# Attention pool of a hybrid encoder: another tile layout, and the last head pair's order of work

## The chip, the cores and the metric

The kernel runs on one core of a Trainium2 chip. The metric is the device time of one execution in microseconds; before the change the median of three runs was 2669.86 us (2669.14 to 2674.19). A core has five engines that run their own instruction streams: PE (TensorE, matmuls; PEld are its weight loads), DVE (VectorE), ACT (ScalarE), POOL (GpSimd) and SP, which here only issues transfers. Operands of matmuls lie in SBUF, results in eight PSUM banks.

## The reference, cut to what matters

Two layers, sequence 1024, width 1024, all in float32:

```
h = rms_norm(x); p = h @ W_in
y_m = 4 heads of a bidirectional mLSTM          (width 512)
y_a = 8 heads x 64 of dilated attention         (width 512):
      rotary q, k; three patterns (window, dilation) = (128,1), (512,4), (2048,16),
      merged by their softmax denominators
x = x + concat(y_m, y_a) @ W_out
x = x + relu(rms_norm(x) @ W_up)^2 @ W_down     (inner width 4096)
```

and a last RMSNorm. The result has the shape of x.

## The kernel before, in words

Everything is kept transposed: 128 channels in the partitions, the sequence along a row. A float32 weight or activation is split into a high part in a faster matmul type and the rest; a product is three matmuls, high x high, high x rest and rest x high. `wsplit` (L77) splits a weight tile: ScalarE casts it (wh, L81), GpSimd subtracts (wl, L83); there are three buffers of each. `operand` and `parts` (L739 to L747) split an activation of 128x1024: ScalarE casts (L742), VectorE subtracts (L743).

A layer runs: norm, gates and four mLSTM heads (pool `mp`), then eight attention heads as four pairs (pool `ap`), then the output projection and four chunks of up and down projection (pool `up`). `ap` and `up` lie over the same stretch of SBUF; a tile of the later pool waits only for those of the earlier pool that it overlaps. Tiles get their places in the order of their first use; `order` (L51) makes the first ones by name ahead of that.

The output projection and the feed-forward part use seven half-size products where eight would be plain (`seven`, L803). Their weights are loaded by `fetch` on SP's queue (L766), and sums of weight blocks are formed by `plus` (L770), an accumulating transfer that GpSimd issues. Two of the seven products of the output projection need only mLSTM outputs; `out_early` (L867) makes them as fillers of the last attention pair, 32 steps of three matmuls each. The other five run after the pair, starting with `products(w1, operand(Y[1][0]))`, then w2, w0, w1 with its second block, and w2 again. `Y[1]` holds the attention outputs, the later half of its tiles those of the last two pairs.

A pair (`a_pair`, L570) has eight steps T of 128 queries. A step makes scores for two heads (`a_scores`), the softmax rows `sm` (VectorE with mask and minimum L604, ScalarE exponential L606, VectorE reciprocal L607 and scaling L608), the weighting of the step before (`take1`, L580), some fillers, and then eight transposes of `sm` (L620), whose results go to `p1` by ScalarE (L622) and, rearranged, to `p23` by VectorE (L623). After the steps come the last `take1` and two output groups `o2` (L640) for the dilated patterns, each added into y by VectorE (L645). `a_vt` transposes the values at the start of a pair (L560). Fillers in the first three pairs are the next pair's q, k and v projection, 48 steps of three matmuls; `a_split` splits the next pair's q and k.

Within the pairs TensorE keeps the written order (`in_order`). Everything else is ordered by a planner that simulates the engines: an instruction goes into its engine's stream when the simulation has it ready, so work without an open dependency can move ahead of where it is written.

Of the kernel before, what the change touches and what calls it, by code (L numbers as in the profile page):

```python
# [12 lines left out]
F32 = mybir.dt.float32  # L13
F32R = mybir.dt.float32r
# [14 lines left out]
NFF = FF // P  # L29
FCH = 8  # L30
NCH = NFF // FCH
POS = 1
SQ = 2
NC = S // P
EPS = 1e-6
# [9 lines left out]
class Trunk:  # L45
# [505 lines left out]
    def a_vt(self, vt, ap, fill):  # L551
        nc = self.nc
        v1 = ap.tile([P, NC + 1, P], F32, name="v1", tag="v1", bufs=1)
        v23 = ap.tile([P, 8, P], F32, name="v23", tag="v23", bufs=1)
        jobs = [(v1, i, vt[:, i * P:(i + 1) * P]) for i in range(NC + 1)]
        jobs += [(v23, 2 * rr + jt, vt[:, 64 + 512 * jt + rr:64 + 512 * (jt + 1):4]) for rr in range(4) for jt in range(2)]
        for lo, n in ((0, 4), (4, 4), (8, 1), (9, 4), (13, 4)):
            pt = self.mx.tile([P, 4, P], F32, name="pt", tag="t", bufs=2)
            for i in range(n):
                nc.tensor.transpose(pt[:, i], jobs[lo + i][2], self.ident)  # L560
            dst, j = jobs[lo][0], jobs[lo][1]
            nc.scalar.copy(dst[:, j:j + n], pt[:, :n])
            fill(1)
        return v1, v23

    def a_pair(self, p, qkv, ops, ap, more, nxt=None, each=5):

        nc = self.nc
        y = self.ytile(MH + p)
        late = None  # L570

        def fill(n):
            for _ in range(n):
                next(more, None)

        def take1(T, o1, p1s):
            for b in range(2):
                for g in range(4):
                    gp = slice(32 * g, 32 * g + 32)
                    nc.tensor.matmul(o1[gp, T % 4], v1[:, T + b, gp], p1s[g // 2][:, b], start=b == 0, stop=b == 1)  # L580
            if T % 4 == 3:
                yv = y[T // 4].rearrange("p (T i r) -> p T r i", T=4, r=4)
                ov = o1.rearrange("p T (r i) -> p T r i", r=4)
                for i in range(4):
                    nc.scalar.copy(yv[:, i], ov[:, i])

        if p == 0:
            fill(2)
            v1, v23 = self.a_vt(qkv[2], ap, fill)
        for T in range(NC):  # L590
            pss = [self.mx.tile([P, 2, 256], F32, name="ps", tag="s", bufs=2) for _ in range(2)]
            self.a_scores(qkv, ops, pss, T)
            if T == 0:
                if p > 0:
                    v1, v23 = self.a_vt(qkv[2], ap, fill)
                p23 = [ap.tile([P, 2, 4, NC, 32], F32, name=f"p23{h}", tag=f"p23{h}", bufs=1) for h in range(2)]
            sms = []
            for h in range(2):
                sm = ap.tile([P, 2, 256], F32, name="sm", tag="sm", bufs=2)
                nm, l = [ap.tile([P, 1], F32, name=n_, tag=n_, bufs=2) for n_ in ("nm", "l")]  # L600
                b0 = 32 * (NC - 1 - T)
                x = self.am[:, b0:b0 + 256]
                mk = bass.AP(x.tensor, x.offset, [x.ap[0], (480 - b0, 2), (1, 256)])
                nc.vector.tensor_tensor_reduce(out=sm, in0=pss[h], in1=mk, op0=ALU.add, op1=ALU.min, scale=-0.125,  # L604
                                               scalar=3e38, accum_out=nm)
                nc.scalar.activation(sm, sm, AF.Exp, scale=-1.0, bias=nm, accum_out=l)  # L606
                nc.vector.reciprocal(l, l)  # L607
                nc.vector.tensor_scalar(out=sm, in0=sm, scalar1=l, scalar2=None, op0=ALU.mult)  # L608
                sms.append(sm)
            if late:  # L610
                take1(*late)
            fill(each if T < NC - 1 else each - 2)
            if T % 4 == 0:
                o1 = self.mx.tile([P, 4, P], F32, name="o1", tag="o", bufs=1)
            p1s = []
            for h in range(2):
                pt = self.mx.tile([P, 4, P], F32, name="pt", tag="t", bufs=2)
                smf = sms[h].rearrange("p g w -> p (g w)")
                for i in range(4):
                    nc.tensor.transpose(pt[:, i], smf[:, i * P:(i + 1) * P], self.ident)  # L620
                p1 = ap.tile([P, 2, P], F32, name="p1", tag="p1", bufs=2)
                nc.scalar.copy(p1, pt[:, 2:4])  # L622
                nc.vector.tensor_copy(p23[h][:, :, :, T], pt[:, 0:2].rearrange("p j (r i) -> p j r i", r=4))  # L623
                p1s.append(p1)
            late = T, o1, p1s
        if nxt and POS == 0:
            self.a_split(nxt, ops)
        fill(1)
        take1(*late)
        if nxt and POS == 1:  # L630
            self.a_split(nxt, ops)
        fill(3)
        for g in range(2):
            o2 = self.mx.tile([P, 2, 256], F32, name="o2", tag="o", bufs=1)
            for rr in range(2):
                r = 2 * g + rr
                for jt in range(2):
                    for g4 in range(4):
                        gp = slice(32 * g4, 32 * g4 + 32)
                        nc.tensor.matmul(o2[gp, rr], v23[:, 2 * r + jt, gp],  # L640
                                         p23[g4 // 2][:, jt, r].rearrange("p T i -> p (T i)"),
                                         start=jt == 0, stop=jt == 1)
            for t in range(2):
                yg = y[t].rearrange("p (j r) -> p r j", r=4)[:, 2 * g:2 * g + 2]
                nc.vector.tensor_tensor(out=yg, in0=o2[:, :, t * P:(t + 1) * P], in1=yg, op=ALU.add)  # L645
            if nxt and POS == 2 + g:
                self.a_split(nxt, ops)
            fill(3 if g == 0 else 48)


    def layer(self, L, xT):
# [36 lines left out]
                    pass  # L688
        with tc.tile_pool(name=f"ax{L}", bufs=1, space=PSUM, reuse_waits="tile") as self.mx:
            with tc.tile_pool(name=f"ap{L}", bufs=1, reuse_waits="tile") as ap:  # L690
                self.order(ap, (("p230", 2 * S, 1), ("rp", HALF, 2), ("qq1", S, 1), ("kk1", S, 1)))
                ks = [ap.tile([P, S + P], F32R, name="ks", tag=f"ks{h}") for h in range(2)]
                qd = [ap.tile([P, S], F32R, name="qd", tag=f"qd{h}") for h in range(2)]
                ql = [ap.tile([P, S], F32R, name="ql", tag=f"ql{h}") for h in range(2)]
# [12 lines left out]
                with self.in_order():  # L707
                    for p in range(AH // 2 - 1):
                        nxt = []
                        self.a_pair(p, qkv, ops, ap, self.a_qkv(L, p + 1, hs, r, tabs, ap, nxt), nxt)  # L710
                        qkv = nxt
                    x2, early = [self.yb("x2") for _ in range(KD)], []
                    for o in range(KD):
                        nc.gpsimd.dma_start(x2[o], (a["x"] if L == 0 else self.xd)[:, o])
                    self.a_pair(AH // 2 - 1, qkv, ops, ap, self.out_early(L, x2, early), each=4)
        with tc.tile_pool(name=f"up{L}", bufs=1, reuse_waits="tile") as self.up:
            self.order(self.up, (("T", S, 4), ("sq", HALF, SQ)))
            with tc.tile_pool(name=f"dn{L}", bufs=1, space=PSUM, reuse_waits="tile") as self.dn:
                acc, op = self.out_proj(early)
                for c in range(NCH):  # L720
                    u, op = self.up_proj(L, c, acc, op)
                    op = self.down_proj(L, c, x2, u, op)
# [79 lines left out]
    def seven(self, src, B, op, take, nxt, early=False, end=None):  # L802
# [2 lines left out]


        (B11, B12), (B21, B22) = B
        T, T3 = [[self.up.tile([P, 2, HALF], F32, name="T", tag="T", bufs=4) for _ in range(2)] for _ in range(2)]
        w0 = self.fetch("w0", src, 0, 0)
        w1 = self.fetch("w1", src, 0, 1)  # L810
        w2 = self.fetch("w2", src, 1, 0)
        addto = lambda w, m, h: lambda q: self.plus(w[q], src(q, m, h))
        if early:
            chain = P5 = None
            for q in range(4):
                addto(w0, 1, 0)(q)
                addto(w2, 1, 1)(q)
                addto(w2, 0, 0)(q)
        else:
            chain = self.products(w0, op, True, then=addto(w0, 1, 0))  # L820
            op = self.operand(B21)
            for q in range(4):
                addto(w2, 1, 1)(q)
            take(1, chain)
# [150 lines left out]
    def final(self, x2):  # L975
# [33 lines left out]
        def end(w, parts):  # L1009
            ws = []  # L1010
            for q in range(4):
                s = self.up.tile([P, 2, 4, P], F32R, name="s", tag="T", bufs=4)
                wh, wl = s[:, 0], s[:, 1]
                nc.scalar.copy(wh, w[q])
                nc.gpsimd.tensor_tensor(out=wl, in0=w[q], in1=wh.bitcast(F32), op=ALU.subtract)
                ws.append((wh, wl))
# [132 lines left out]
```

## Time and profile before

| | |
|---|---|
| runs | 2669.86 us median, 2669.14 to 2674.19 |
| profiled execution | 2674.39 us, span 2672.6 us, mean granted TensorE clock 0.976 |
| PE busy | 2475.1 us (93%) |
| PEld busy | 1958.6 us (73%) |
| DVE busy | 1962.1 us (73%) |
| ACT busy | 1266.9 us (47%) |
| POOL busy | 1406.8 us (53%) |
| transfers | 214.08 MB, mean 80 GB/s |

The span is the part of an execution from its first to its last instruction. Busy time of an engine leaves out waits, branches and the issue of transfers on SP. In layer 0 the attention pairs run from some 385 to 626 us, in layer 1 from some 1707 to 1947 us; the last pair is 560 to 626 and 1883 to 1947, and the output projection follows it.

### The profile page before, as it was taken

The page shows a single profiled execution, that of the slowest core. Times are in us where ns is not written, and L with a number is a line of the kernel's source. Part 1 is how long each engine was busy: PE and PEld are TensorE (multiplying, and loading weights), DVE is VectorE, ACT ScalarE, POOL GpSimd, SP SyncE. Part 2 cuts the span into 40 slices and gives each one's busy share as a digit, 9 for nine tenths or more (in the row PEclk, how much of TensorE's full clock was granted, in tenths as well). Part 3 has the DMA queues.
Part 4 walks back from the last instruction along what each step waited for, and adds up shares of the span by engine and source line. Part 5 has one row for each costly group of instructions (what it writes and reads, how often), then busy time and mean ns, then how long its engine had stood idle before and what let it go on. Part 6 is the DMA issues. An engine that isn't in the chain of part 4 may idle for free. (4 is left out here: it accounts for less than half of the span.)

```text
span 2672.6 us, 36085 instructions
## 1 busy us (share of the span) xinstructions
PE 2475.1 (93%) x13508; PEld 1958.6 (73%) x13508; DVE 1962.1 (73%) x2456; ACT 1266.9 (47%) x2076; POOL 1406.8 (53%) x1135
## 2 busy tenths in 40 slices
PE   7989989996999999999989898999979999999997
PEld 5777766664778878788767777666657788887876
DVE  7877666586877686967878776566768867768587
ACT  5433344453654545445444334444446445454544
POOL 5333322235576677766654333223266666767765
PEclk9999999998999999999999999999989999999999
DMA  3001100035455455555321111001264555556553
GB/s 133 28 28 32 36 30 25 21 111 127 103 111 107 100 110 112 108 112 115 87 71 32 32 32 38 21 25 51 78 142 95 113 113 107 110 103 111 110 102 85
DMA packets 113327, 214.08 MB, mean 80 GB/s; under 512 B 13424, under 2 KB 15616, under 8 KB 113152
## 3 DMA queue, kind: packets, MB, share of 16 engines
q0 software_dynamic: 46912, 93.06, 21.0%
q1 hardware_dynamic: 66240, 118.71, 14.6%
q8 instruction: 107, 1.75, 0.3%
q14 instruction: 68, 0.56, 0.1%
HBM read 203.33 MB, written 8.39 MB: 79 GB/s over the span
## 5 line engine op out<-in xcount | busy, mean ns | idle before, releaser
L83 POOL TENSOR_TENSOR wl<-w,wh 128x512 fp32r<-128x512 f32 x484 | 777.9, 1627 | 287.7 <-ACT wh L81 286.9
L794 PE MATMUL ph<-b,wh 128*128 128x512 f32 x2240 | 694.3, 391 | 5.9 <-ACT wh L81 5.9
L81 ACT CAST wh<-w 128x512 fp32r<-128x512 f32 x484 | 298.4, 618 | 433.6 <-PE ph L794 118.8
L794 PEld LDWEIGHTS ph<-b,wh 128*128 128x128 f32 x2240 | 422.5, 189 | 95.2 <-ACT wh L81 7.8
L794 PE MATMUL ph<-b,wl 128*128 128x512 f32 x1120 | 441.0, 394 | 13.4 <-POOL wl L83 13.1
L83 POOL TENSOR_TENSOR wl<-wr,wh 128x512 fp32r<-128x512 f32 x132 | 200.1, 1517 | 464.1 <-ACT wh L81 379.2
L794 PE MATMUL pj<-b,wh 128*128 128x512 f32 x1224 | 382.9, 394 | 12.5 <-ACT wh L81 12.5
L91 PE MATMUL pj<-hh,wh 128*128 128x512 f32 x896 | 371.4, 415 | 17.5 <-DVE z L174 10.6
L93 PE MATMUL pj<-hh,wl 128*128 128x512 f32 x896 | 359.5, 401 | 0.9 <-POOL rs L213 0.6
L92 PE MATMUL pj<-hl,wh 128*128 128x512 f32 x896 | 359.8, 402 | 0.0
L743 DVE TENSOR_TENSOR b<-T,b 128x1024 fp32r<-128x1024 f32 x148 | 247.6, 1677 | 135.2 <-ACT b L742 131.5
L794 PEld LDWEIGHTS pj<-b,wh 128*128 128x128 f32 x1224 | 232.0, 190 | 63.8 <-ACT wh L81 14.2
L794 PEld LDWEIGHTS ph<-b,wl 128*128 128x128 f32 x1120 | 211.3, 189 | 67.8 <-POOL wl L83 24.4
L794 PE MATMUL pj<-b,wl 128*128 128x512 f32 x612 | 241.4, 394 | 17.8 <-POOL wl L83 17.8
L91 PEld LDWEIGHTS pj<-hh,wh 128*128 128x128 f32 x896 | 172.4, 192 | 67.0 <-issue 13.9
L93 PEld LDWEIGHTS pj<-hh,wl 128*128 128x128 f32 x896 | 171.9, 192 | 36.7 <-POOL rs L213 1.0
L92 PEld LDWEIGHTS pj<-hl,wh 128*128 128x128 f32 x896 | 172.6, 193 | 30.0 <-issue 0.5
L742 ACT CAST b<-T 128x1024 fp32r<-128x1024 f32 x148 | 155.5, 1051 | 38.4 <-PE ph L794 13.6
L770 POOL DMA_DIRECT2D w<-w_down x128 | 115.9, 936 | 75.7 <-PE pj L794 27.8
L794 PEld LDWEIGHTS pj<-b,wl 128*128 128x128 f32 x612 | 116.2, 190 | 46.2 <-POOL wl L83 22.2
L606 ACT ACTIVATE sm<-sm,nm 128x512 f32<-128x512 f32 x128 | 91.7, 718 | 113.8 <-DVE nm L604 113.8
L770 POOL DMA_DIRECT2D w<-w_up x128 | 113.3, 911 | 59.7 <-POOL wl L83 22.4
(256 smaller groups left out, 4296.7 us busy)
## 6 DMA issues: line engine op xcount, KB each, us to landing
w<-w_up SPq DMA_DIRECT2D x128, 256.0 KB, 2.7
w<-w_up POOLq DMA_DIRECT2D x128, 256.0 KB, 4.1
w<-w_down SPq DMA_DIRECT2D x128, 256.0 KB, 2.7
w<-w_down POOLq DMA_DIRECT2D x128, 256.0 KB, 4.3
wr<-w_in SPq DMA_DIRECT2D x116, 256.0 KB, 2.7
w<-w_out SPq DMA_DIRECT2D x32, 256.0 KB, 5.1
w<-w_out POOLq DMA_DIRECT2D x32, 256.0 KB, 6.1
wr<-w_out SPq DMA_DIRECT2D x16, 256.0 KB, 2.8
```

The costliest lines, as they stand in the source:

```text
L81: nc.scalar.copy(wh, raw)
L83: nc.gpsimd.tensor_tensor(out=wl, in0=raw, in1=wh.bitcast(F32), op=ALU.subtract)
L91: nc.tensor.matmul(ps, wh[:, j, :], xh[:, sl], start=start, stop=False)
L92: nc.tensor.matmul(ps, wh[:, j, :], xl[:, sl], start=False, stop=False)
L93: nc.tensor.matmul(ps, wl[:, j, :], xh[:, sl], start=False, stop=stop)
L606: nc.scalar.activation(sm, sm, AF.Exp, scale=-1.0, bias=nm, accum_out=l)
L742: nc.scalar.copy(hi, src)
L743: nc.vector.tensor_tensor(out=lo, in0=src, in1=hi.bitcast(F32), op=ALU.subtract)
L770: self.nc.gpsimd.dma_start(w, src, accum_op=ALU.add)
L794: nc.tensor.matmul(out, a[:, k, :], b, start=new and k + i == 0, stop=k + i == 5, skip_group_check=not new)
```

## The change

The pools are laid out otherwise, the last pair makes its scores one step ahead, and the fillers are spread otherwise. Places are in columns of four bytes per partition, as the order of tiles gives them:

| columns | `ap` before | `up` before | `ap` after | `up` after |
|---|---|---|---|---|
| 0 to 2048 | p230 | T | p230 | T3 |
| 2048 to 3072 | rp | T | rp | w1 (first two tiles) |
| 3072 to 4096 | qq1 | T | qq0 | w1 (last two) |
| 4096 to 5120 | kk1 | sq | kk0 | T |
| 5120 to 6144 | ks0 | w0 | ks0 | T |
| 6144 to 8192 | ks0, ks1, qd0 | w0, w1 | ks0, ks1, qd0 | w2 |
| 8192 to 10240 | qd0, qd1, ql0 | w1, w2 | qd0, qd1, ql0 | w0 |
| 10240 to 11264 | ql0, ql1 | w2 | ql0, ql1 | sq |

The last pair uses qq1 and kk1, which move behind ql1; qq0 and kk0 are those of the pair before. `rp` held temporaries of the rotary step and now also the `sm` of odd steps of the last pair.

In `a_pair` the softmax part of a step becomes `weights(T)`, the transposes `turn(T, sms)`. In the last pair `weights(T + 1)` stands before the fillers and transposes of step T, and the second head's copy into `p23` goes to ScalarE. Fillers of the last pair: none in `a_vt`, three in each of eight steps, two before the last `take1`, three after it and three between the output groups (before: five, four per step and the rest where it came until the 32 were used up). Pairs 1 and 2 have five in the last step (before three), and two, one and one at the end (before one, three and three); all pairs have three in `a_vt` (before five), and pair 0 four ahead of it (before two). The second output group takes its bank from the tag "t", not "o". In the output projection w0 is fetched last, and its accumulating transfers stand behind those of w2.

```diff
-        for lo, n in ((0, 4), (4, 4), (8, 1), (9, 4), (13, 4)):
+        for lo, n, m in ((0, 4, 1), (4, 4, 1), (8, 1, 0), (9, 4, 1), (13, 4, 0)):
...
-            fill(1)
+            fill(m)
...
+        def weights(T):
             pss = [self.mx.tile([P, 2, 256], F32, name="ps", tag="s", bufs=2) for _ in range(2)]
             self.a_scores(qkv, ops, pss, T)
...
-                sm = ap.tile([P, 2, 256], F32, name="sm", tag="sm", bufs=2)
+                sm = ap.tile([P, 2, 256], F32, name="sm", tag="rp" if last and T % 2 else "sm", bufs=2)
...
+        def turn(T, sms):
...
-                nc.vector.tensor_copy(p23[h][:, :, :, T], pt[:, 0:2].rearrange("p j (r i) -> p j r i", r=4))
+                dst, src = p23[h][:, :, :, T], pt[:, 0:2].rearrange("p j (r i) -> p j r i", r=4)
+                if not last or h == 0:
+                    nc.vector.tensor_copy(dst, src)
+                else:
+                    nc.scalar.copy(dst, src)
...
+        if p == 0:
+            fill(4)
+            v1, v23 = self.a_vt(qkv[2], ap, fill)
+        sms = weights(0)
+        if p > 0:
+            v1, v23 = self.a_vt(qkv[2], ap, (lambda n: None) if last else fill)
+        p23 = [ap.tile([P, 2, 4, NC, 32], F32, name=f"p23{h}", tag=f"p23{h}", bufs=1) for h in range(2)]
+        for T in range(NC):
+            if not last:
+                if T > 0:
+                    sms = weights(T)
+            elif T + 1 < NC:
+                ahead = weights(T + 1)
+            if late:
+                take1(*late)
+            fill((5 if T < NC - 1 or p > 0 else 3) if not last else 3)
+            if T % 4 == 0:
+                o1 = self.mx.tile([P, 4, P], F32, name="o1", tag="o", bufs=1)
+            late = T, o1, turn(T, sms)
+            if last:
+                sms = ahead
+        fill(2)
+        take1(*late)
+        if nxt:
             self.a_split(nxt, ops)
-        fill(3)
+        fill(1 if not last else 3)
         for g in range(2):
-            o2 = self.mx.tile([P, 2, 256], F32, name="o2", tag="o", bufs=1)
+            o2 = self.mx.tile([P, 2, 256], F32, name="o2", tag=("o", "t")[g], bufs=g + 1)
...
-            fill(3 if g == 0 else 48)
+            fill((1 if not last else 3) if g == 0 else 48)
...
-                self.order(ap, (("p230", 2 * S, 1), ("rp", HALF, 2), ("qq1", S, 1), ("kk1", S, 1)))
+                self.order(ap, (("p230", 2 * S, 1), ("rp", HALF, 2), ("qq0", S, 1), ("kk0", S, 1), ("ks0", S + P, 1),
+                                ("ks1", S + P, 1), ("qd0", S, 1), ("qd1", S, 1), ("ql0", S, 1), ("ql1", S, 1),
+                                ("qq1", S, 1), ("kk1", S, 1)))
...
-            self.order(self.up, (("T", S, 4), ("sq", HALF, SQ)))
+            self.order(self.up, (("T3", S, 2), ("w1", HALF, 4), ("T", S, 2), ("w2", HALF, 4), ("w0", HALF, 4),
+                                 ("sq", HALF, SQ)))
...
-        T, T3 = [[self.up.tile([P, 2, HALF], F32, name="T", tag="T", bufs=4) for _ in range(2)] for _ in range(2)]
-        w0 = self.fetch("w0", src, 0, 0)
+        T, T3 = [[self.up.tile([P, 2, HALF], F32, name="T", tag=tag, bufs=2) for _ in range(2)] for tag in ("T", "T3")]
+        if not early:
+            w0 = self.fetch("w0", src, 0, 0)
...
         if early:
             chain = P5 = None
+            w0 = self.fetch("w0", src, 0, 0)
+            for q in range(4):
+                addto(w2, 1, 1)(q)
+                addto(w2, 0, 0)(q)
             for q in range(4):
                 addto(w0, 1, 0)(q)
-                addto(w2, 1, 1)(q)
-                addto(w2, 0, 0)(q)
```

## Rows read from the trace of the kernel before

**Rows 1.** Chain of waits: start us, us, what; feed-forward part of layer 1.
```profile
2062.64 32.64 PE ph L794 x144
```

**Rows 2.** Waits of PE, 1883 to 1981 (layer 1): us in total, times, longest.
```profile
PE pj L794 <- POOL wl L83: 6.3, 1, 6.3
PE pj L794 <- ACT wh L81: 6.2, 1, 6.2
PE ph L794 <- ACT wh L81: 2.9, 1, 2.9
PE pt L620 <- DVE sm L608: 2.3, 2, 1.9
PE pt L620 <- DVE l L607: 1.8, 1, 1.8
PE o L640 <- DVE y L645: 1.3, 1, 1.3
PE o L640 <- ACT y L585: 1.2, 1, 1.2
PE ph L794 <- POOL wl L83: 0.6, 1, 0.6
```

**Rows 3.** Waits of PE, 560 to 660 (layer 0), the first of four alike.
```profile
PE pj L794 <- POOL wl L83: 6.2, 1, 6.2
```

**Rows 4.** Timeline, handover of layer 1: start us, us, work, [idle before <-releaser].
```profile
1932.38 1.11 PE L620 MATMUL pt<-ident,sm 128*128 128x128 f32 x8
...
1933.76 34.15 SPq L766 DMA_DIRECT2D w<-w_out  x16
...
1934.29 1.11 PE L548 MATMUL ps<-kk,qq 64*32 64x256 f32 x16
...
1944.75 1.93 PE L640 MATMUL o<-p,v 128*32 128x256 f32 x32 [1.33 <-DVE y L645]
1946.74 1.12 DVE L645 TENSOR_TENSOR y<-o,y 128x256 f32<-128x256 f32 x2 [2.14 <-PE o L640]
...
1951.29 1.04 ACT L742 CAST b<-T 128x1024 fp32r<-128x1024 f32 x1 [1.23 <-DVE T L752]
1952.24 1.66 ACT L81 CAST wh<-w 128x512 fp32r<-128x512 f32 x3
...
1952.94 9.85 POOL L83 TENSOR_TENSOR wl<-w,wh 128x512 fp32r<-128x512 f32 x3 [11.56 <-ACT wh L81]
...
1957.99 1.22 DVE L743 TENSOR_TENSOR b<-T,b 128x1024 fp32r<-128x1024 f32 x1
1960.38 0.80 PE L794 MATMUL pj<-b,wl 128*128 128x512 f32 x1 [6.25 <-POOL wl L83]
...
1962.74 3.50 POOL L770 DMA_DIRECT2D w<-w_out  x4
...
1975.15 0.62 ACT L81 CAST wh<-w 128x512 fp32r<-128x512 f32 x1 [5.14 <-DMA w<-w_out]
```

**Rows 5.** Tile w, 1933.7 to 1941: twelve fetches, four accumulating transfers.
```profile
DMA to landing us min/median/max: 2.9/7.5/11.5
```

**Rows 6.** Busy time by window: PE, PEld, DVE, ACT, POOL, granted clock, DMA, GB/s.
```profile
1883.00:1947.00 64.00, 56.71 (x545) 38.83 (x537) 47.38 (x113) 26.77 (x68) 13.82 (x16) 0.97 0.35 89
1946.70:2022.00 75.30, 59.30 (x241) 47.66 (x242) 53.80 (x52) 40.76 (x60) 47.12 (x37) 0.89 0.56 120
1946.70:2038.10 91.40, 72.13 (x290) 56.43 (x290) 69.01 (x63) 54.28 (x82) 59.27 (x47) 0.91 0.58 118
```

**Rows 7.** Line L770, 1880 to 1920: three accumulating transfers in the last pair.
```profile
DMA to landing us min/median/max: 3.9/4.1/4.1
```

**Rows 8.** Groups of ACT, 1883 to 1947: busy us, mean ns, idle before.
```profile
L562 ACT COPY v<-pt 128x512 f32<-128x512 f32 x4 | 2.3, 583 | 3.1 <-PE pt L560 3.1
```

**Rows 9.** Waits of PE, 1700 to 1882 (pairs 0 to 2 of layer 1).
```profile
PE pt L620 <- DVE sm L608: 11.8, 6, 3.6
PE o L640 <- DVE y L645: 2.3, 3, 1.3
```

More of the change, by code (lines that the diff above doesn't have):

```diff
@@ L31 @@
 NCH = NFF // FCH
-POS = 1
 SQ = 2
@@ L562, in a_vt, with a_pair @@
             nc.scalar.copy(dst[:, j:j + n], pt[:, :n])
-            fill(1)
+            fill(m)
         return v1, v23
-    def a_pair(self, p, qkv, ops, ap, more, nxt=None, each=5):
+    def a_pair(self, p, qkv, ops, ap, more, nxt=None):
         nc = self.nc
         y = self.ytile(MH + p)
-        late = None
+        late, last = None, nxt is None
         def fill(n):
@@ L585, in take1 @@
                     nc.scalar.copy(yv[:, i], ov[:, i])
[L587 to L590, printed above, removed]
+        def weights(T):
             pss = [self.mx.tile([P, 2, 256], F32, name="ps", tag="s", bufs=2) for _ in range(2)]
             self.a_scores(qkv, ops, pss, T)
[L593 to L596, printed above, removed]
             sms = []
             for h in range(2):
-                sm = ap.tile([P, 2, 256], F32, name="sm", tag="sm", bufs=2)
+                sm = ap.tile([P, 2, 256], F32, name="sm", tag="rp" if last and T % 2 else "sm", bufs=2)
                 nm, l = [ap.tile([P, 1], F32, name=n_, tag=n_, bufs=2) for n_ in ("nm", "l")]
@@ L609, in a_pair @@
                 sms.append(sm)
[L610 to L614, printed above, removed]
+            return sms
+        def turn(T, sms):
             p1s = []
@@ L622, in a_pair @@
                 nc.scalar.copy(p1, pt[:, 2:4])
-                nc.vector.tensor_copy(p23[h][:, :, :, T], pt[:, 0:2].rearrange("p j (r i) -> p j r i", r=4))
-                p1s.append(p1)
-            late = T, o1, p1s
-        if nxt and POS == 0:
-            self.a_split(nxt, ops)
[L628 to L631, printed above, removed]
-        fill(3)
+                dst, src = p23[h][:, :, :, T], pt[:, 0:2].rearrange("p j (r i) -> p j r i", r=4)
[3 more added lines that the diff above has]
+                    nc.scalar.copy(dst, src)
+                p1s.append(p1)
+            return p1s
+        if p == 0:
[22 more added lines that the diff above has]
+        if nxt:
+            self.a_split(nxt, ops)
+        fill(1 if not last else 3)
         for g in range(2):
-            o2 = self.mx.tile([P, 2, 256], F32, name="o2", tag="o", bufs=1)
+            o2 = self.mx.tile([P, 2, 256], F32, name="o2", tag=("o", "t")[g], bufs=g + 1)
             for rr in range(2):
@@ L645, in a_pair @@
                 nc.vector.tensor_tensor(out=yg, in0=o2[:, :, t * P:(t + 1) * P], in1=yg, op=ALU.add)
-            if nxt and POS == 2 + g:
-                self.a_split(nxt, ops)
-            fill(3 if g == 0 else 48)
+            fill((1 if not last else 3) if g == 0 else 48)
     def layer(self, L, xT):
@@ L714, in layer @@
                         nc.gpsimd.dma_start(x2[o], (a["x"] if L == 0 else self.xd)[:, o])
-                    self.a_pair(AH // 2 - 1, qkv, ops, ap, self.out_early(L, x2, early), each=4)
+                    self.a_pair(AH // 2 - 1, qkv, ops, ap, self.out_early(L, x2, early))
         with tc.tile_pool(name=f"up{L}", bufs=1, reuse_waits="tile") as self.up:
-            self.order(self.up, (("T", S, 4), ("sq", HALF, SQ)))
+            self.order(self.up, (("T3", S, 2), ("w1", HALF, 4), ("T", S, 2), ("w2", HALF, 4), ("w0", HALF, 4),
+                                 ("sq", HALF, SQ)))
             with tc.tile_pool(name=f"dn{L}", bufs=1, space=PSUM, reuse_waits="tile") as self.dn:
@@ L1011, in end @@
             for q in range(4):
-                s = self.up.tile([P, 2, 4, P], F32R, name="s", tag="T", bufs=4)
+                s = self.up.tile([P, 2, 4, P], F32R, name="s", tag=("T", "T3")[q // 2], bufs=2)
                 wh, wl = s[:, 0], s[:, 1]
```

## Prediction

> **What bounds the kernel now.** I read the page's engine table first, then TensorE's waits stretch by stretch, then the timeline where they are longest, then busy time by window. The table shows TensorE busy for most of the span, so the kernel can only win where TensorE waits, or runs at its lower clock. In the chain of waits the feed-forward part shows 144 matmuls of 128x512 in 32.64 us without a break, 0.2267 us from start to start [rows 1]; that is my price for a matmul. The largest breaks stand at one place per layer, the handover from the last attention pair to the output projection. In layer 1 TensorE waits there 6.2 us for a cast of a weight (wh), 6.3 us for the rest of the same weight (wl), then 2.9 and 0.6 us for the next product's weights [rows 2], 16.0 us in sum; layer 0 repeats it, its wait for wl is 6.2 us [rows 3].
>
> The timeline says why [rows 4]. The last score matmuls of the pair start at 1934.29 and end at 1935.40, and only at 1933.76 does SP begin the twelve weight fetches, since their slots lay on the score operands; with the first accumulating transfers they land up to 11.5 us after issue [rows 5]. The last matmuls of the pair end at 1946.7. VectorE then works without a gap to 1959.2, two adds of the output and ten differences and subtractions in SBUF that had no slot or operand before. ScalarE casts the first weights at 1952.24, behind casts of these operands. GpSimd begins wl at 1952.94 and needs 9.85 us for three; TensorE gets the first of them at 1960.38, 1.2 us after VectorE's run has ended. Meanwhile four accumulating transfers stand behind those wl in GpSimd's queue and are issued from 1962.74, so the second product's weights are cast only at 1975.15, after 5.14 us of waiting on a transfer.
>
> The five steps of the projection in this stage are 240 matmuls, 240 x 0.2267 = 54.4 us at full rate. From 1946.7 to their end at 2022.0 they take 75.3 us: 20.9 us lost, 16.0 of them waits and 4.9 at the lower clock (granted 0.89 over the window [rows 6]: part of the time at 1.2 GHz, after the waits).
>
> **The change part by part** (per layer; rows of layer 1).
>
> *Layout and order of loads.* After the change half of w1 lies on the key/query tiles of the pair before (free early), half on the tile "rp", which now holds softmax rows of the last odd step; w2 and w0 lie on score operands as before, T on kk0 and ks0. From the last scores to the end of the pair there lay 11.3 us, of which 4.4 us waits (1.9, 1.2, 1.3 [rows 2]), so 6.9 us of work. After it there lie the same 6.9 us, eight transposes more (1.1 us [rows 4]) and 14 fillers of three matmuls (3+3+2+3+3, 0.68 us each, 9.5 us): 17.5 us. So w2 and w0 are fetched 17 us before the pair ends. The "rp" half of w1 comes free at the last transposes, 9.3 us before the end (8 fillers 5.4, two output groups of 1.93). With the median landing of 7.5 us all are there in time. The eight accumulating transfers of w2 are two in series, 4.1 us landing each in the last pair [rows 7]: 17.5 - 7.5 - 8.2, ready about when the pair ends, and needed 48 matmuls (10.9 us) later. The issues themselves (0.87 us each on GpSimd by the row of four, twelve of them) go into a stretch where GpSimd is busy 13.8 of 64 us [rows 6].
>
> So at the end of the pair w1 is split for three of four tiles (three wh/wl buffers), the differences into T are done, and the first six matmuls have operands from older pairs. What is late next: the operand of the last pair itself, an add 0.56, a cast 1.04, a subtraction 1.22 us and the handoffs between them, some 3.4 us after the end against 1.4 us of matmuls that don't need it: 2 us at most, less if the planner puts other products between. Then wl of the fourth tile: its buffer comes free 2.7 us after the end and VectorE then has some 8 us of subtractions (this operand 1.1, an unused one 2.3, the next difference and its operand 4.6). I take 2 us for that; bounds are 0 (GpSimd gets in between) and 6.3 (as now [rows 2]). Left of 20.9 us: 4. **Gain 16.9 us.**
>
> *A rule on this.* The first of the three wl lasts from 1952.94 to TensorE's start at 1960.38, 7.4 us under VectorE's run; the other two share the 2.4 us left [rows 4]. The Trainium skill, "SBUF — State Buffer", section "Who interferes with whom", says that a VectorE operation with two SBUF inputs and a GpSimd operation that reads SBUF exclude one another, and that the second to issue blocks until the first finishes. By that the wl would have waited for one subtraction, 1.1 us, not for six; the trace disagrees on the length. By the rule the residue would be 3 us and not 4, and the gain 1 us more a layer.
>
> *Last pair.* Waits now: 1.8 and 2.3 us on softmax rows, 1.2 on a ScalarE copy, 1.3 on the adds between the two output groups, 6.6 in sum [rows 2], and about 1 us of low clock after them (granted 0.97 over 64 us [rows 6] could be worth 1.9; I take half). Scores a step ahead give the softmax a whole step; the 32 fillers reach to the end instead of running out in step 7; the second output group gets a bank of its own. VectorE is busy 47.4 of 64 us there [rows 6] and gives one of two strided copies per step to ScalarE (busy 26.8), so on the mean it is not the limit; in the first half, where each four fillers bring four adds into x and not two, the mean says little. New: the 17 transposes of the values stand without fillers; five copies of 0.58 us and less [rows 8] pace them, some 3 us with handoffs, of which TensorE's own work hides perhaps half: 1.5 us. Another 1.5 us I leave for waits in the dense steps (bounds 0 and the 4.1 of today on softmax rows). **Gain 7.6 - 3 = 4.6 us.**
>
> *Pairs 0 to 2.* Waits now 14.1 us, 11.8 on softmax rows and 2.3 on the adds between output groups [rows 9]. The 2.3 go. Pairs 1 and 2 have two more fillers in step 7 (1.4 us of cover each, 2.8). Against it there is one filler (0.68) where three stood ahead of the first output group, which waits for ScalarE's copies (the 1.2 us of rows 2 came with none): 0.7 us each, 2.1; and fewer fillers among the value transposes, 0.5 each in two pairs. 2.3 + 2.8 - 2.1 - 1.0: **gain 2 us**, bounds -2 and 6.
>
> *Behind the handover.* The same VectorE work must fit in less time. From the end of the pair to the sum of squares at 2038.1 it is busy 69.0 of 91.4 us [rows 6]. With 16.9 us less it has 74.5, of which some 5 us of work has gone ahead into the pair (four operations of 1.2 us into T and the older half of the operand): 64 of 74.5. Tight, with GpSimd contending; I take 2.5 us given back (bounds 0 and 10).
>
> *At nothing:* T3 and T as two tags (the same four buffers), the s tiles, the moved constant, w0 fetched last: it is used third, 22 us after the handover. If that cover were gone, w0 would cost its landing, 7.5 us at most.
>
> **Sum:** 16.9 + 4.6 + 2 - 2.5 = 21.0 a layer, 42.0 in both. The profiled execution took 2674.39 us (span 2672.6 and 1.8 around it); 2674.4 - 42.0 = 2632.4. The median of the runs is 2669.86, 4.5 lower; by the same difference 2627.9, and I say 2628.
>
> **Rivals.** *VectorE bounds the stretch up to the norm* (18%). For it: 64 of 74.5 us, and GpSimd wants the same memory ports, as rows 4 show from its side. Against it: in the feed-forward part the same pair runs beside a full TensorE. Price 7 to 10 given back instead of 2.5: 2628 + 2 x 6 = 2640, up to 2645.
> *Half the handover stays* (14%): the "rp" half of w1 and ScalarE's order make wl late again, behind VectorE's run. For it: 7.4 us once already. Against: 9.3 us of lead. The 6.3 us wait and its low clock stay, 9 us less gain a layer: 2646.
> *Everything goes* (11%): handover and last pair without residue, nothing given back, pairs 6: 20.9 + 7.6 + 6 = 34.5 would be the limit; some 30 a layer give 2610.
> *It does not do what it says* (3%): the planner leaves the fetches where they are; only pairs and banks remain, 2 us a layer, 2666.
> *Slower* (4%): the accumulating transfers, now inside the pair, stand in GpSimd's queue ahead of a filler's wl. TensorE keeps its written order there, so it waits for the filler while GpSimd waits for a fetch. The wait is at worst a fetch and two accumulating transfers in series, 11.5 + 4.1 + 4.1 = 19.7 us [rows 5, 7]; with 4.9 us of low clock behind it 24.6 a layer, more than the 21.0 gained: 2669.9 + 7 = 2677. It decides from 21 us of loss per layer. Against it: wl of the fillers are due before the last scores, and the fetches start only there.
> The Trainium skill, "SBUF — State Buffer", section "SBUF: two separate sides", has a rule of that kind: transfers issued from GpSimd starve while VectorE runs operations that take the shared ports. The three accumulating transfers now in the last pair, amid softmax scaling, land in 4.1 us, no later than 0.2 us behind the fastest [rows 7]; by that row it doesn't bite here, and I add no chance for it.
>
> **How the numbers follow.** Forecast 50%, 2617 to 2640 by the bounds of its residues. Range 2610 to 2650: outside lie the far half of "everything goes", the edges of the two middle rivals, and the last two. A measurement of this kernel can tell 0.2%, 5.3 us. Faster than 2664.5: all but the last two, 0.93; within: 0.03; slower: 0.04.
>
> **What would show it.** Right: w_out fetches issued before the last pair's second output group; the two waits of six us gone and less than 5 us of waiting between the pair's end and the end of the projection; the granted clock there near 1.0; no wait for the adds between output groups. Wrong: a wl over 4 us at the handover; a wait of more than 5 us at the norm's matmuls; fillers waiting for wl in the last pair; a wait for copies above 1 us ahead of each first output group.

## The result and the profile after

The changed kernel took 2657.1 us (median of 6 runs, 2649.64 to 2660.53) beside 2670.69 us for the kernel before: ratio 0.9944, interval [0.9929, 0.9958]. It is faster, by 14 us and not by 42; the time lies above the predicted range. The profiled execution has a span of 2651.2 us, 21.4 less than before.

The table cuts the span at two places per layer: E, where the last output matmul of the last pair ends, and N, where the matmuls with ones of the norm behind the projection start again after their wait for VectorE's sum acc (both from the timeline, in us). "Start to E" and "N to E" hold the pairs, "E to N" the handover and the projection.

| kernel | start to E, layer 0 | E to N, layer 0 | N to E, layer 1 | E to N, layer 1 | rest |
|---|---|---|---|---|---|
| before | 626.3 | 90.3 | 1230.2 | 91.5 | 634.5 |
| after | 614.6 | 89.6 | 1221.3 | 91.6 | 634.2 |
| e1_pair_only | 612.4 | 91.8 | 1218.9 | 92.1 | 634.3 |
| e2_layout_only | 623.5 | 91.8 | 1226.0 | 89.7 | 636.7 |
| e3_rows_kk0 | 615.0 | 92.8 | 1214.6 | 91.5 | 636.9 |
| e4_wh_first | 612.5 | 84.4 | 1220.1 | 82.7 | 635.4 |
| e5_order_all | 611.8 | 82.5 | 1217.8 | 86.3 | 637.6 |
| e6_pair_wh_first | 614.1 | 83.3 | 1216.9 | 82.4 | 634.5 |
| e7_pair_order_all | 613.8 | 83.7 | 1219.7 | 81.6 | 637.1 |
| e8_order_fill | 616.3 | 82.8 | 1220.8 | 82.6 | 635.4 |
| e9_before_wh_first | 623.2 | 82.3 | 1225.0 | 82.8 | 636.6 |
| e10_t_after | 612.5 | 79.8 | 1220.1 | 80.9 | 633.5 |

After against before: all that was won was won ahead of E, 11.7 and 8.9 us. E to N, from which the prediction took 14.4 us a layer, moved by -0.6 and +0.1.

The waits of TensorE in the last pair and the handover of layer 1, which answer to [rows 2] (us in total, times, longest):
```profile
PE pj L812 <- ACT wh L80: 4.0, 1, 4.0
PE ph L812 <- ACT wh L80: 3.8, 1, 3.8
PE ph L812 <- DVE x L818: 3.4, 1, 3.4
PE pt L559 <- ACT v L561: 1.9, 1, 1.9
PE pj L812 <- POOL wl L82: 1.0, 1, 1.0
```
Layer 0 has the same five (4.0, 2.8, 3.6, 1.9 and 1.0 us), where 6.2 us for wl stood before [rows 3]. The pair's own waits (6.6 us) are down to 1.9 us in the value transposes, and TensorE waits for no add between the output groups any more. At the first product 5.0 us are left of 12.5. But the wait at the second product (ph for wh) is 3.8 us where it was 2.9, and a wait of 3.4 us for VectorE's adds is new. Pairs 0 to 2 of layer 1, against [rows 9]:
```profile
PE pt L613 <- DVE sm L602: 8.5, 5, 2.9
PE o L657 <- ACT y L585: 2.4, 3, 1.5
PE pt L559 <- ACT v L561: 1.1, 2, 0.6
```
The timeline of the handover in layer 1, against [rows 4]:
```profile
1914.83 21.17 SPq L784 DMA_DIRECT2D w<-w_out  x15
...
1923.55 1.93 PE L657 MATMUL o<-p,v 128*32 128x256 f32 x32
...
1926.19 1.04 ACT L760 CAST b<-y 128x1024 fp32r<-128x1024 f32 x1 [7.85 <-DVE y L662]
1926.59 1.22 DVE L770 TENSOR_TENSOR T<-y 128x1024 f32<-128x1024 f32 x1
...
1928.85 1.66 ACT L80 CAST wh<-w 128x512 fp32r<-128x512 f32 x3
...
1929.51 0.73 PE L812 MATMUL pj<-b,wh 128*128 128x512 f32 x2 [4.02 <-ACT wh L80]
1929.54 6.10 POOL L82 TENSOR_TENSOR wl<-w,wh 128x512 fp32r<-128x512 f32 x3 [18.34 <-ACT wh L80]
...
1931.26 0.80 PE L812 MATMUL pj<-b,wl 128*128 128x512 f32 x1 [1.02 <-POOL wl L82]
...
1935.58 2.62 POOL L788 DMA_DIRECT2D w<-w_out  x3
...
1947.92 0.62 ACT L80 CAST wh<-w 128x512 fp32r<-128x512 f32 x1 [5.32 <-DMA w<-w_out]
```
The fetches begin at 1914.8, 10.7 us before E at 1925.5, and not 17. The first two tiles of w1 lie on `rp`, and w2 and w0 stand behind them in SP's one queue, so all twelve wait for the last transposes; the waits of SP's queue, 1912 to 1925:
```profile
SPq L784 <- PE pt L613: 3.3, 1, 3.3
```
The row to look at is the cast of `b` at 1926.19: ScalarE sat idle for 7.85 us until VectorE's `y`, the result of the pair's last matmuls. Only behind it, and behind a cast of T, do the casts of w1 come, without a wait of their own: the weights were there (fetched from 1914.8, landed at most 6.0 us after issue). The differences into T, which VectorE makes, also begin only behind `y`, at 1926.59. GpSimd in turn sat 18.3 us until the first wh. When the weights landed decides nothing here; where their casts stand in ScalarE's order does. The kernel before has the same row:
```profile
1947.38 1.04 ACT L742 CAST b<-y 128x1024 fp32r<-128x1024 f32 x1 [5.95 <-DVE y L645]
```
Busy time of layer 1 by window, against [rows 6] (us; busy PE, PEld, DVE, ACT, POOL; granted clock, DMA share, GB/s). First the kernel after, cut at the second product's first matmul, then the kernel before with the same cut:
```profile
1925.50:1948.60 23.10, 14.27 (x49) 10.95 (x49) 19.97 (x15) 9.15 (x13) 15.20 (x13) 0.83 0.61 125
1948.60:2000.80 52.20, 47.01 (x192) 37.60 (x193) 43.16 (x38) 31.26 (x49) 31.45 (x27) 0.95 0.56 118
1925.50:2017.00 91.50, 74.40 (x290) 57.36 (x290) 78.92 (x63) 53.49 (x82) 59.56 (x51) 0.93 0.60 120
```
```profile
1946.70:1975.80 29.10, 13.74 (x48) 10.38 (x48) 18.52 (x17) 9.83 (x14) 18.07 (x12) 0.77 0.62 128
1975.80:2022.00 46.20, 45.56 (x193) 37.27 (x194) 35.29 (x35) 30.93 (x47) 29.05 (x25) 0.96 0.51 115
```
Up to the second product the changed kernel is 6.0 us shorter (23.1 against 29.1), and it loses just that behind it (52.2 against 46.2; the cuts are the second product's first matmul and the end of the projection). At the first product wh stands behind one cast of T and not two, and TensorE has the first wl 1.7 us after GpSimd began it (1931.26), not 7.4. From E to N VectorE is busy 78.9 us with 63 instructions, where 63 took 69.0 us: single ones are drawn out beside GpSimd. Some of them, kernel after:
```profile
1957.31 3.63 DVE L761 TENSOR_TENSOR b<-T,b 128x1024 fp32r<-128x1024 f32 x1
1957.71 2.15 POOL L82 TENSOR_TENSOR wl<-w,wh 128x512 fp32r<-128x512 f32 x1
...
1960.75 4.05 POOL L82 TENSOR_TENSOR wl<-w,wh 128x512 fp32r<-128x512 f32 x3
1960.87 4.48 DVE L107 TENSOR_TENSOR acc<-acc,sq 128x512 f32<-128x512 f32 x1
```
The subtraction into b takes 3.63 us (1.22 elsewhere), the add into acc 4.48 (0.73 at 1949.7); the add into x behind it comes late, and TensorE waits 3.4 us. Drawn-out adds into acc are not what is new: the kernel before has one of 4.48 us too, at 2033.6. By kind, in layer 1, the subtractions into b take some 5.5 us more than before and the operations that write T some 4; the adds into acc take 0.8 more.

### The profile page after: what moved, and what is told of

Read it like the earlier page. It is cut to its first block, busy times and chain, and to the rows that moved or that the text cites. A ratio compares the mean times of both kernels' runs of the same rounds, so it can differ in the third digit from the quotient of the medians.

```text
span 2651.2 us, 36031 instructions
## 1 busy us (share of the span) xinstructions
PE 2476.5 (93%) x13508; PEld 1958.3 (74%) x13508; DVE 1994.6 (75%) x2440; ACT 1269.2 (48%) x2092; POOL 1395.1 (53%) x1135
## 5 line engine op out<-in xcount | busy, mean ns | idle before, releaser
L82 POOL TENSOR_TENSOR wl<-w,wh 128x512 fp32r<-128x512 f32 x484 | 768.8, 1610 | 311.5 <-ACT wh L80 311.1
L90 PE MATMUL pj<-hh,wh 128*128 128x512 f32 x896 | 368.9, 412 | 18.0 <-DVE z L173 10.8
L761 DVE TENSOR_TENSOR b<-T,b 128x1024 fp32r<-128x1024 f32 x148 | 253.0, 1714 | 114.3 <-ACT b L760 110.9
L600 ACT ACTIVATE sm<-sm,nm 128x512 f32<-128x512 f32 x128 | 91.6, 717 | 131.5 <-DVE nm L598 131.5
```

The lines of the kernel that those rows point to most:

```text
L82: nc.gpsimd.tensor_tensor(out=wl, in0=raw, in1=wh.bitcast(F32), op=ALU.subtract)
L90: nc.tensor.matmul(ps, wh[:, j, :], xh[:, sl], start=start, stop=False)
L761: nc.vector.tensor_tensor(out=lo, in0=src, in1=hi.bitcast(F32), op=ALU.subtract)
```

## Experiments

Three theories. **S**: the slots come free too late or SP's queue is blocked (w1 on `rp` waits for the last odd softmax rows, and the other fetches stand behind it). **Q**: the order of instructions in the streams of ScalarE and VectorE holds the handover, wherever the weights lie. **V**: VectorE and GpSimd together bound E to N.

**e1_pair_only and e2_layout_only**: the change in two halves. e1 has the diff of `a_pair` and `a_vt` alone; e2 has the rest (both `order` lists, the tags T and T3, w0 fetched last).

> The changed pairs (scores a step ahead, fillers, banks) with the tile layout and the load order of before. The stretch from the end of the last pair to the sum of squares (E to norm) took 91.4 us before and 91.5 after. If the layout is worth nothing as it stands, this run equals the changed kernel: about 2657 us, E to norm 91 +- 2 us in layer 1. If the layout does help and the pairs' change hides it, this run is slower than 2662.

Measured: 2655.05 us, ratio 0.9949 [0.9934, 0.9964].

> The layout and the load order of the change with the pairs of before; rp is then free from the pair before, so the fetches of w1 can leave long before the end of the pair. Theory S (slots: the fetch of w1 on rp blocks SP's queue): E to norm shrinks by 6 us or more a layer, time about 2658 or less. Theory Q (queue order: the new pool's casts, differences and accumulating transfers stand behind the pair's last output in the streams of ScalarE, VectorE and GpSimd, whatever the slots): E to norm 90 +- 2, time 2671 +- 4. Theory V (VectorE and GpSimd, which hold each other up, bound the stretch up to the norm): 90 +- 2 as well.

Measured: 2671.56 us, ratio 1.0014 [1.0004, 1.0024]. All of the gain comes from the pairs; the layout is worth nothing or a little less. e2 has the waits of the kernel after at the handover (4.0, 3.8 and 3.6 us in layer 1), so the layout and the order of loads do move the waits, but E to N stays at 91.8 and 89.7. Which part of the pairs' change won (scores a step ahead, fillers, the second bank) no run separates. In e1, with the layout of before but scores a step ahead, the fetches begin 20 us before E (1923.1), and the waits are still those of [rows 2]. Waits and timeline of e1, layer 1:
```profile
PE pj L809 <- ACT wh L80: 6.3, 1, 6.3
PE pj L809 <- POOL wl L82: 6.2, 1, 6.2
PE ph L809 <- ACT wh L80: 2.4, 1, 2.4
```
```profile
1903.19 6.95 SPq L781 DMA_DIRECT2D w<-w_out  x12
...
1923.82 1.04 ACT L757 CAST b<-y 128x1024 fp32r<-128x1024 f32 x1 [7.85 <-DVE y L662]
...
1928.73 1.66 ACT L80 CAST wh<-w 128x512 fp32r<-128x512 f32 x3
```

**e3_rows_kk0**: S by itself, the slot of w1 free early.
```diff
-                sm = ap.tile([P, 2, 256], F32, name="sm", tag="rp" if last and T % 2 else "sm", bufs=2)
+                if last and T % 2:
+                    if h == 0:
+                        both = ap.tile([P, 2, 2, 256], F32, name="sm", tag="kk0", bufs=1)
+                    sm = both[:, h]
```


> The changed kernel with the odd softmax rows on kk0 in place of rp, so all of w1 has free slots when the last pair begins. Theory S: SP fetches w1 early in the last pair, the waits of 4.0 and 1.0 us for wh and wl at the handover go, E to norm 80 us or less, time about 2637. Theory Q: the fetches leave early but wh is cast only after the operand of the last pair; E to norm 91 +- 2, time 2657 +- 5. Theory V: waits may move, E to norm 91 +- 2.

Measured: 2653.25 us, ratio 0.9947 [0.9934, 0.9961], E to N 92.8 and 91.5. The first four fetches begin at 1888.1, 34 us before E, and land at most 4.1 us after issue; the waits stay 4.0, 3.8, 3.4 and 1.0. S falls.

**e4_wh_first**: Q, the casts of three w1 tiles written ahead of the last pair's operand and kept ahead of it in ScalarE's stream.
```diff
         if early:
...
+            pre = [self.wsplit(w) for w in w1[:3]]
+            op = [self.parts(B21[0])]
+            with self.tc.issue_after(self.cast.ins):
+                op.append(self.parts(B21[1]))
...
-        ps = self.products(w1, op)
+        ps = self.products(w1, op, pre=pre)
```


> The changed kernel with the casts of three w1 tiles put ahead of the cast of the last pair's operand in ScalarE's stream. Theory Q: the 4.0 us wait for wh goes, wl is done under the pair's end; the handover gets 4 to 6 us shorter a layer and most of it reaches the norm: E to norm 86 to 88 us, time about 2648. Theory V: the wait for wh goes, but VectorE's subtractions or the adds into x wait instead, E to norm 90 to 92, time 2655 to 2659. Theory S: the casts wait for the transfers, no change.

Measured: 2640.0 us, ratio 0.9904 [0.9884, 0.9924]; E to N is 5.2 and 8.9 us shorter than in the kernel after. Q holds, with more than it expected (86 to 88, 2648). V as a hard bound falls, since the stretch got shorter; VectorE is busy 67 of 82.7 us in it.

**e6_pair_wh_first and e9_before_wh_first**: the edit of e4 on e1 (changed pairs, layout of before), and on the kernel before itself.

> The changed pairs and the casts of w1 ahead, but the pool's layout and the order of loads of the kernel before: e4_wh_first without the layout. Theory Q with the layout as its condition: with w1 landing late (PE for wh 6.3 us, for wl 6.2 us in e1_pair_only) the casts cannot be early whatever the order, the stretch from the last output matmul to the norm stays at 88 to 92 us and the time at 2650 to 2655. Rival, the order alone: the stretch is that of e4_wh_first, 83 to 85 us, and the time 2640.

Measured: 2633.36 us, ratio 0.9874 [0.986, 0.9888].

> The kernel before with one edit: the casts of three w1 tiles ahead of the cast of the last pair's operand in ScalarE's stream; its pairs, its layout and its order of loads stay. The fetches of w_out begin 13 us before the pair's last output matmul there and landed in 2.9 to 11.5 us. Theory Q (order alone held the handover): the stretch from the last output matmul to the norm's matmul falls from 90 to 92 us to 81 to 83, as in e6_pair_wh_first, and the time by 18 us: ratio 0.993. The prediction's reading (the slots came free too late, so the fetches were late): the waits of about 6 us for wh and wl stay, less than 3 us a layer are won, ratio 0.998 or more.

Measured: 2650.88 us, ratio 0.9929 [0.991, 0.9948]. The order alone does it: 91.8 and 92.1 (e1) become 83.3 and 82.4 (e6), and in the kernel before 90.3 and 91.5 become 82.3 and 82.8. e9 keeps SP's order and, but for one exchange a layer, GpSimd's, and the fetches lead E (1930.4) by 13 us as they did. The planner also moves ScalarE's casts of T and VectorE's operations: the four differences into T now stand ahead of the subtraction into b, and TensorE waits 4.1 and 2.8 us a layer for that b. So VectorE's new order brings waits and is not where the gain comes from. Timeline of e9, layer 1:
```profile
1917.50 12.29 SPq L766 DMA_DIRECT2D w<-w_out  x15
...
1924.98 1.66 ACT L81 CAST wh<-w 128x512 fp32r<-128x512 f32 x3
...
1925.69 3.75 POOL L83 TENSOR_TENSOR wl<-w,wh 128x512 fp32r<-128x512 f32 x3 [0.48 <-ACT wh L81]
1928.52 1.93 PE L640 MATMUL o<-p,v 128*32 128x256 f32 x32 [1.35 <-DVE y L645]
1930.38 0.73 PE L794 MATMUL pj<-b,wh 128*128 128x512 f32 x2
```
The casts stand 5.5 us ahead of E, the three wl take 3.75 us (9.85 in [rows 4]), and the first product follows the pair without a wait. With the order mended the layout of the change is no help either: e4 has it and is at 0.9904, e6 has not and is at 0.9874.

**e5_order_all and e7_pair_order_all**: on e4 and e6, the rest of the order.
```diff
+            with self.tc.issue_after(self.rest.ins):
+                for j in range(2):
+                    self.nc.vector.tensor_tensor(out=T[j], in0=B11[j], in1=B12[j], op=ALU.subtract)
+            op2 = self.negsum(T, B22)
```


> The changed kernel with the whole order mended: the casts of three w1 tiles ahead (as in e4_wh_first), and besides the operand of B11 minus B12 that nothing reads is left out, the subtractions into T stand behind the last pair's own operand on VectorE, and the operand of the sum into T is started before the tiles of w1's products. In e4_wh_first the stretch from the end of the last pair's output matmuls to the norm's matmul was 84.4 and 82.7 us, with waits of 2.8 us (PE for VectorE's b, which stood behind 4.6 us of subtractions into T), 3.8 to 5.6 us (PE for ScalarE's b) and 1.3 us (wl). Theory Q (the order in the streams is what holds the handover): the 2.8 us go, the 3.8 to 5.6 us fall to 0 to 2, the stretch becomes 76 to 79 us, the time 2640 - 2 x 5 = 2630 (2625 to 2634). Theory V (VectorE and GpSimd together bound the stretch): VectorE was busy 67 of 82.7 us; leaving out two casts and two subtractions gives 2 to 3 us a layer at most and the rest comes back as waits for GpSimd's wl: 2635 to 2640.

Measured: 2637.99 us, ratio 0.9892 [0.9879, 0.9905]. Q's 2630 is missed; the time is the one V gave, though not by its waits: the 2.8 us are down to 0.6, but in the second product of layer 1 a wait of 6.7 us for VectorE's b and one of 2.7 us for wh came, not one for wl.

> e6_pair_wh_first with the rest of the order mended as in e5_order_all, still in the layout and load order of the kernel before. If the layout is what the order needs: 2640 to 2650, with waits for wh or wl of w1 left at the start of the stretch. If the order alone does it: as e5_order_all, 2630, and the layout would be worth nothing in any order.

Measured: 2632.55 us, ratio 0.9876 [0.9863, 0.9888], as e6. The two waits of e6 for b (4.1 and 2.8 us) are gone, waits of 2.7 and 2.1 us for wl stand in their place in layer 1; E to N is 83.7 and 81.6 against 83.3 and 82.4.

**e8_order_fill**: e5 with `fill(2)` ahead of the output groups, and the value transposes with 1, 0, 0, 1, 0 fillers in all pairs.

> e5_order_all with the fillers spread otherwise: in all pairs alike a filler fewer inside the transposes of v, one more ahead of the output matmuls (2 in place of 1; in the last pair 2 and 2 in place of 3 and 3, and one each at three places of its transposes). The stalls of the changed kernel that this aims at: the output matmuls wait 2.4 us a layer for ScalarE's y (3x, up to 1.5), and the last pair waits 1.9 us in its transposes. If a filler covers its own length there, 1 to 2 us a layer go: 2 to 4 us below e5_order_all. Rival: the filler taken out leaves the same wait earlier, no difference within 2 us.

Measured: 2648.32 us, ratio 0.9929 [0.9916, 0.9941], slower than e5. In pairs 0 to 2 of layer 0 the 2.4 us for ScalarE's y are gone, but the waits on softmax rows rise from 8.5 to 10.6 us and 1.6 us for their sums are new. So the filler moved the wait, as the rival says, but the rival's size (no difference within 2 us) is missed: the median lies 10 us above e5. The profiled execution is the fastest of the six (2639.63, e5's 2637.79), so its trace can't show where the 10 us are, and that stays open.

**e10_t_after**: e7 without the line of `op2`, the sum into T where it was.

> e6_pair_wh_first with the four subtractions into T behind the last pair's own subtraction on VectorE, without the operand that nothing reads, and with the sum into T where it was. In e6_pair_wh_first TensorE waits 4.1 and 2.8 us for VectorE's b, behind 4.6 us of subtractions. Theory Q: those waits go, the stretch falls from 82 to 77 us, 2 x 5 = 10 us less, 2623. Theory V as a soft bound (VectorE has 67 us of work there and GpSimd's wl stretch beside it, so a wait taken from one place comes back in another): waits for wl of 3 to 5 us take their place, as in e7_pair_order_all, and the time stays within 3 us of 2633.

Measured: 2628.45 us, ratio 0.9846 [0.9825, 0.9867], the fastest here, 41 us under the kernel before by the ratio. Its waits in layer 1, last pair and projection:
```profile
PE pj L129 <- DVE acc L107: 2.1, 1, 2.1
PE pt L559 <- ACT v L561: 1.9, 1, 1.9
PE ph L809 <- POOL wl L82: 1.9, 3, 0.6
PE ph L809 <- DVE b L758: 1.8, 1, 1.8
PE ph L809 <- ACT wh L80: 1.2, 1, 1.2
```
E to N is 3.5 and 1.5 us shorter than in e6, half of the 5 a layer that Q expected. V as a soft bound is missed too: TensorE waits 1.9 us for wl in layer 1, not 3 to 5, and the time is 4.9 us under that of e6, not within 3 of 2633. The waits for b fell from 6.9 us a layer to 2.6 and 2.1. The two intervals just overlap, so how much e10 wins over e6 stays open.

## Why the prediction was wrong

**The step that failed** is in "Layout and order of loads": "So at the end of the pair w1 is split for three of four tiles (three wh/wl buffers), the differences into T are done". It took the casts to follow the landing of the weights. They follow ScalarE's order, in which the cast of the last pair's operand, bound to E, stood ahead of them before and after; the first of w1 is cast at 1928.85, 3.4 us behind E. Nor are the differences into T done at E: VectorE begins the first of them at 1926.59, behind the pair's `y`. The trace of the kernel before held the contradiction. The fetches of w1 are the fifth to eighth of the twelve (tile w, 1935.55 to 1937.1):
```profile
L766 SPq DMA_DIRECT2D w<-w_out x4: 430/430/438, 1935.6 to 1937.0; - x4
DMA to landing us min/median/max: 4.9/5.3/6.6
```
So w1 lay in SBUF by 1943.6, 8.6 us before its first cast at 1952.24. That cast has no releaser in [rows 4], and the rows of ScalarE just ahead of it waited for VectorE. I took for a late load what was a late turn. e1 (lead of 20 us, same waits), e3 (slot free early, nothing) and e9 (lead of 13 us as before, the two waits of 6 us gone) settle it.

**The gain of 16.9 us** came to 0.6 and -0.1. The changed kernel's first product had 7.5 us of waits less. Of that 6.0 us were left at the second product: the accumulating transfers are still issued behind the wl of w1 (1935.6, 10.1 us after E), and the second product's wh sits 5.3 us until a transfer has landed. Behind it the 6.0 us were lost again, with VectorE's operations drawn out. TensorE's waiting from E to the end of the projection, which was to be under 5 us, is 12.2 us in the rows shown. Against the kernel before, mending the order gave 7.0 to 9.1 us a layer in e9 and e6, 10.5 and 10.6 in e10. So with the right mechanism, too, 14.4 (16.9 less the 2.5 given back) would have been 4 us too much: the stretch still holds 67 us of work on VectorE, and a wait that goes comes back in part one place later (e5, e7).

**Pairs.** The terms of the last pair (4.6) and of pairs 0 to 2 (2) were 6.6 a layer; from the first `kk` scores (ps<-kk,qq) of pair 0 to E the kernel after needs 10.8 and 6.9 us less. Cut at the first `kk` scores of each pair: the last pair won 7.0 and 4.6 us, pairs 1 and 2 together 4.7 and 3.4, pair 0 lost 0.9 and 1.1. The value transposes wait 1.9 us (1.5 assumed) and the first output groups wait for ScalarE's copies, up to 1.5 us, as written (0.7 each). Waits on softmax rows fell further than assumed, from 11.8 to 8.5.

**Given back.** The prediction took 5 us of VectorE's work to go ahead into the pair, which would leave 64 us in 74.5, and 2.5 us of the gain to come back. None went ahead: VectorE has 63 instructions from E to N before and after, and they got longer, 69.0 to 78.9 us, without the handover having got shorter.

**Rivals.** "It does not do what it says" named the outcome (only pairs and banks remain) but put them at 2 us a layer and for another reason, fetches that stay where they were; they moved. "Half the handover stays" named ScalarE's order in half a sentence and priced it at 9 us a layer; lost were all 16.9. "VectorE bounds the stretch" puts 7 to 10 us in place of 2.5, which gives 2637 to 2643 and not up to 2645; e4, e9 and e6 got the stretch shorter, so it is no hard bound. The last pair shows no wait of TensorE for a filler's wl.

**The rule weighed.** The Trainium skill, "SBUF — State Buffer", section "Who interferes with whom", says that a VectorE operation with two SBUF inputs and a GpSimd operation that reads SBUF contend, and that the one issued second waits until the first has finished. In e9 three wl without VectorE's run beside them take 3.75 us, against 9.85 in [rows 4], which agrees that one holds up the other. It does not agree on the length: in e1 a single wl lasts 7.33 us beside six operations of VectorE, and in the kernel after an add on VectorE that begins at 1960.87, 0.1 us behind the first of three wl, lasts 4.48 us instead of 0.73, until the third has ended.

## What to carry to other kernels

Before an earlier load or a freer slot is priced, look at the row of the consumer that comes first after it: if it has no wait on the transfer, and the row ahead of it on the same engine waits for something else, the order of that engine is what has to change. Try the order alone first: three casts put ahead of one gave 19 to 20 us by the ratios (e9 on the kernel before, e6 on e1), and a new layout of two pools gave nothing (e2). Where a busy engine stands behind a wait, the gain is what its next wait leaves of it: in e10 the waits for b fell by 4.3 and 4.8 us against e6, and the stretch got 3.5 and 1.5 us shorter.

## What the runs showed of the hardware

The same three subtractions of 128x512 on GpSimd took 3.75 us with VectorE nearly idle (e9), 6.10 in the kernel after and 9.85 in [rows 4]. The reverse was not expected: an add of 128x512 on VectorE took 0.73 us, and 4.48 us beside three wl and the issue of one accumulating transfer on GpSimd. A wl by itself is enough to draw it out: at 1982.0 in the kernel after the same add took 1.78 us beside one wl, with no transfer being issued. What the issue adds to the 4.48 us was not separated.
